# FFN up products by Strassen's algorithm, and the down products after them

## The chip, the core and the metric
One core of a Trainium2 chip runs the kernel. The metric is the device time of one execution in microseconds. Five engines matter: TensorE (PE, with its weight loads PEld), VectorE (DVE), ScalarE (ACT), GpSimd (POOL) and the DMA queue of SyncE (SP). Each works through its own instructions in order and waits for the others by semaphores.

## The reference
One layer over 1024 frames of 1024 channels, in float32; both FFNs have 2816 inner channels:

```
x = x + 0.5 * swiglu(rmsnorm(x, norm_ffn1), wg1, wu1, wd1)
h = rmsnorm(x, norm_mix)
x_m, z_m, x_r, y_r = split(h @ w_in)
mixed = [rmsnorm(mlstm_group(x_m, z_m)), rmsnorm(rglru_group(x_r, y_r))]
x = x + mixed @ w_out
x = x + 0.5 * swiglu(rmsnorm(x, norm_ffn2), wg2, wu2, wd2)
out = rmsnorm(x, norm_final)
swiglu(x, wg, wu, wd) = (silu(x @ wg) * (x @ wu)) @ wd
```

The change is in the two `swiglu` and in how x passes into and out of them.

## The kernel before
Channels lie on the 128 partitions, frames on the free axis: x is eight tiles of 128 x 1024 (`xs`, two tiles of four), each in two halves of 512 frames. A float32 value is split into two parts, hi by a cast on ACT (L105) and lo = value - hi by DVE or POOL (L106); a product is the sum of three passes, hi*hi, hi*lo, lo*hi (`PASSES`), each a matmul of 128 x 128 weights against 128 x 512 values. So a projection of one row of 128 inner channels is 2 halves x 8 tiles x 3 = 48 matmuls (`project`, L285).

An FFN has 22 rows of 128 inner channels. `up_pair` does two of them: gate by L285, times the frames' reciprocal root mean square `rb` on DVE (L330), silu on ACT (L331), times `rb` on POOL (L332), up by L285, the product on DVE (L334) and the split of the result. The norm is late: the products run on x times the gain (`hT`, made by `split_scaled`, L109 on ACT and L110 on DVE), and `rb` is applied to their results. `rb` comes from the squares of x added up in `acc` (L175 on ACT, L177 on POOL or DVE), four small matmuls for each half (L146), a division on DVE (L149, `ms`), a power on POOL (L138), two parts on DVE (L153, L154), two diagonal matrices on DVE (L162), two matmuls that spread the result over the partitions (L165) and a copy on ACT (L166). `defer` and `tick` set where in PE's order these matmuls come: a number of product groups later.

`down` is interleaved with `up_pair`: after every second pair of rows, the rows of the pair before are multiplied with the down weights (L302) and added to x in place (L345); the last call takes four rows. Weights are loaded by SP into `raw` and split into `wu`. In FFN1 the loads of x and the first weights set the pace; in FFN2, `hT` is made while the output projection of the mixer still runs, and L285 matmuls stand between its parts and the statistics.

Of the kernel before, what the change touches and what calls it, by code (L numbers as in the profile page):

```python
# [12 lines left out]
P = 128  # L13
# [20 lines left out]
def hymba_block_kernel(ctx: ExitStack, tc, xT, chv, qkv, kblk, wgate, bgate, up1, dn1, up2, dn2,  # L34
# [13 lines left out]
    r_d = [dram.tile([P, T], F32, name=f"r_d{i}") for i in range(NK)]  # L48
    m_d = dram.tile([H, T], F32, name="m_d")
# [48 lines left out]
    def t2(pool):  # L98
        return pool.tile([P, 512], F32, tag="t2", name="t2", bufs=4)
# [81 lines left out]
    def defer(n, fn):  # L181

        waiting.append([n, fn])
# [16 lines left out]
    class Norm:  # L200
# [3 lines left out]
        def __init__(self, pool, gain, late=False):  # L204
            self.pool, self.gain, self.late, self.acc = pool, gain, late, [[], []]
            self.hT = self.rb = None

# [73 lines left out]

    def project_half(ps, w, hT, half):
# [35 lines left out]
    def ffn(pool, xs, norm, up, dn, after, ahead=(), load_next=lambda: None, last_pieces=halves):  # L318
        hT, rb = norm.hT, norm.rb
        ahead = list(ahead)  # L320

        def up_weights(i):
            return ahead[i] if i < len(ahead) else weights(up[i])

        def up_pair(g):
            res = []
            for f in (2 * g, 2 * g + 1):
                pg = project(up_weights(2 * f), hT)
                s = t4(pool)
# [3 lines left out]
                pu = project(up_weights(2 * f + 1), hT)  # L333
                nc.vector.tensor_tensor(out=s, in0=s, in1=pu, op=ALU.mult)  # L334
                gt = pair(pool, "u8")
                split(gt[:, 0], gt[:, 1], s)
                res.append(gt)
            return res

        def down(fs, acts, last):  # L340
            pieces = last_pieces if last else halves

            def apply(m, h, ps):
                xt = row(xs, m)[:, pieces[h]]
                nc.vector.scalar_tensor_tensor(out=xt, in0=ps, scalar=0.5, in1=xt,  # L345
                                               op0=ALU.mult, op1=ALU.add)
                if last:
                    after(m, h)
            rows = [weights(dn[f]) for f in fs]
            if last:  # L350
                load_next()
            contract(rows, acts, apply, last, pieces)

        last = NF // 2 - 1
        pending = []
        for g in range(last + 1):
            pending += up_pair(g)
            if g == 0:
                open_psum(2, 4)
            if 0 < g < last:  # L360
                down((2 * g - 2, 2 * g - 1), pending[:2], False)
                pending = pending[2:]
        down(range(2 * last - 2, 2 * last + 2), pending, True)


# [6 lines left out]
    open_psum(3, 2)  # L372
    with tc.tile_pool(name="f1", bufs=4, reuse_waits="tile") as pool:
        norm = Norm(nrm, "n1", True)
        ahead = []
        for h in range(2):
            for m in range(NK):
                nc.sync.dma_start(out=row(xs, m)[:, half_of(h)], in_=xT[m, :, half_of(h)])
                norm.scale(xs, m, h)
                if h == 0 and m % 4 == 0:  # L380
                    ahead.append((weights if m else weights_by_half)(up1[m // 4]))
        for h in range(2):
            for m in range(NK):
                norm.square(xs, m, h, 1, (nc.gpsimd, nc.vector)[h])
# [739 lines left out]
```

## Time and profile before

| what | us |
| --- | --- |
| median of 3 runs | 2249.03 |
| lowest and highest | 2248.6, 2249.38 |
| the profiled execution | 2248.25 |
| its span, first to last instruction | 2246.5 |
| PE busy | 2202.3 (98%) |
| DVE busy | 1110.4 (49%) |
| ACT busy | 663.4 (30%) |
| POOL busy | 365.2 (16%) |

The granted clock of TensorE is 0.997 of full speed in the mean. A busy time is the sum over an engine's instructions, also where it works in the shadow of another; what counts is the engine that the end of a stage waits for. FFN1 runs from the start to about 730 us, the mixer to about 1490 us, FFN2 from there to the end.

### The profile page before, as it was taken

Reading aid. Unit: us, or ns where it says so; the run is one execution under the profiler, and the core shown is the slowest. Engines: PE = TensorE matmul, PEld = TensorE weight load, DVE = VectorE, ACT = ScalarE, POOL = GpSimd, SP = SyncE. Lnnn points to the kernel's source line nnn. Section 1 sums busy time; section 2 is a strip of 40 time slices with the busy share of each in tenths; the row PEclk is TensorE's granted clock in tenths of the full one; section 3 lists DMA queues with packets and bytes.
Section 4 is the critical chain, followed back from the end, with each engine's and each line's share of the span. In section 5 each row is a group of like instructions: output and inputs, shape, how many; then the busy total and the mean of one; then the engine's idle time right before and its main releaser. Section 6 shows DMA issues by size and latency. Waiting matters only on the chain.

```text
span 2246.5 us, 24257 instructions
## 1 busy us (share of the span) xinstructions
PE 2202.3 (98%) x10102; PEld 1816.0 (81%) x10102; DVE 1110.4 (49%) x1567; ACT 663.4 (30%) x865; POOL 365.2 (16%) x217
## 2 busy tenths in 40 slices
PE   7999999999999999999999999999999999999998
PEld 5888888888888788878788887777888888888887
DVE  6334344333443645665538999873433334343334
ACT  5111111111112445555546554242111111111114
POOL 3000000000002301232311113431000000000004
PEclk9999999999999999999999999999999999999999
DMA  4111111111112312132246322211111111111102
GB/s 172 55 47 47 48 47 40 54 57 47 47 57 72 116 40 66 64 103 85 85 169 207 104 66 76 71 33 56 47 38 57 47 49 55 47 47 38 57 19 75
DMA packets 62069, 152.12 MB, mean 68 GB/s; under 512 B 5380, under 2 KB 24068, under 8 KB 60936
## 3 DMA queue, kind: packets, MB, share of 16 engines
q1 hardware_dynamic: 61960, 150.58, 20.6%
q8 instruction: 79, 1.29, 0.2%
q14 instruction: 30, 0.25, 0.0%
HBM read 124.85 MB, written 25.71 MB: 67 GB/s over the span
## 4 chain that ended last, share of the span: by engine, by line
PE 86%; DVE 7%; issue 2%; POOL 2%; ACT 1%; DMA 0%; SPq 0%; POOLq 0%; DVEq 0%; ACTq 0%
PE bank_a L285 54%; PE bank_b L302 23%; PE bank_s L302 3%; PE bank_a L531 2%; PE bank_s L808 1%; PE bank_b L837 1%; DVE wu L106 1%; DVE xs L962 1%; DVE hT L110 1%; DVE t L239 1%; DVE w L952 1%; POOL r L138 1%; PE bank_b L634 0%; PE bank_b L619 0%; PE bank_b L616 0%
## 5 line engine op out<-in xcount | busy, mean ns | idle before, releaser
L285 PE MATMUL bank_a<-hT,wu 128*128 128x512 f32 x5712 | 1313.3, 390 | 14.6 <-ACT wu L105 6.2
L285 PEld LDWEIGHTS bank_a<-hT,wu 128*128 128x128 f32 x5712 | 1070.3, 188 | 245.1 <-DVE hT L110 8.1
L302 PE MATMUL bank_b<-u,wu 128*128 128x512 f32 (+1 forms) x2496 | 555.2, 382 | 2.5 <-DVE xs L345 1.3
L302 PEld LDWEIGHTS bank_b<-u,wu 128*128 128x128 f32 x2496 | 456.9, 189 | 95.8 <-DVE xs L962 3.3
L105 ACT CAST wu<-raw 128x1024 fp32r<-128x1024 f32 (+1 forms) x183 | 188.5, 1045 | 1118.5 <-PE bank_a L285 548.1
L345 DVE SCALAR_TENSOR_TENSOR xs<-bank_b,xs 128x512 f32<-128x512 f32 (+1 forms) x328 | 220.1, 677 | 178.7 <-PE bank_b L302 177.1
L332 POOL TENSOR_TENSOR t<-t,rb_late 128x1024 f32<-128x1024 f32 x44 | 105.4, 2396 | 1202.4 <-ACT t L331 1202.4
L106 DVE TENSOR_TENSOR wu<-raw,wu 128x1024 fp32r<-128x1024 f32 (+1 forms) x183 | 226.5, 1247 | 56.8 <-ACT wu L105 56.8
L334 DVE TENSOR_TENSOR t<-t,bank_a 128x1024 f32<-128x1024 f32 x44 | 53.8, 1222 | 366.2 <-PE bank_a L285 362.6
L330 DVE TENSOR_TENSOR t<-rb_late,bank_a 128x1024 f32<-128x1024 f32 x44 | 53.7, 1221 | 311.4 <-PE bank_a L285 309.9
L302 PE MATMUL bank_s<-wu 128*128 128x512 f32 x384 | 97.9, 396 | 3.1 <-ACT wu L105 2.3
L302 PEld LDWEIGHTS bank_s<-wu 128*128 128x128 f32 x384 | 69.5, 188 | 18.6 <-ACT wu L105 3.2
L497 DVE SCALAR_TENSOR_TENSOR t<-bank_a,ch,t 128x1023 f32<-128x1023 f32 (+2 forms) x48 | 61.4, 1278 | 46.0 <-ACT t L494 45.5
L177 POOL TENSOR_TENSOR acc<-acc,t 128x512 f32<-128x512 f32 (+1 forms) x47 | 63.5, 1351 | 109.7 <-ACT t L175 59.3
L105 ACT CAST u<-t 128x1024 fp32r<-128x1024 f32 (+1 forms) x56 | 57.2, 1021 | 26.1 <-DVE t L334 13.5
L808 PE MATMUL bank_s<-q,k 128*128 128x512 f32 (+3 forms) x288 | 61.0, 345 | 0.6 <-DVE q L106 0.6
L837 PE MATMUL bank_b<-v,pc 128*128 128x258 f32 x432 | 61.0, 284 | 0.0
L837 PEld LDWEIGHTS bank_b<-v,pc 128*128 128x128 f32 x432 | 58.0, 190 | 2.7
L106 DVE TENSOR_TENSOR u<-t,u 128x1024 fp32r<-128x1024 f32 x44 | 53.8, 1222 | 1.1 <-ACT u L105 1.1
L808 PEld LDWEIGHTS bank_s<-q,k 128*128 128x128 f32 x288 | 47.7, 189 | 7.8 <-DVE q L106 1.4
L962 DVE TENSOR_TENSOR xs<-xs,bank_b 128x512 f32<-128x512 f32 x64 | 42.7, 681 | 16.5 <-PE bank_b L302 16.3
L331 ACT ACTIVATE t<-t 128x1024 f32<-128x1024 f32 x44 | 46.7, 1062 | 7.6 <-DVE t L330 7.6
(207 smaller groups left out, 1366.3 us busy)
## 6 DMA issues: line engine op xcount, KB each, us to landing
raw<-in_up_dram SPq DMA_DIRECT2D x87, 512.0 KB, 3.6
raw<-in_dn_dram SPq DMA_DIRECT2D x44, 512.0 KB, 3.5
raw<-in_win_dram SPq DMA_DIRECT2D x32, 512.0 KB, 3.6
v_d<-u SPq DMA_DIRECT2D x8, 1024.0 KB, 3.8
v<-v_d SPq DMA_DIRECT2D x16, 512.0 KB, 7.0
raw<-in_wout_dram SPq DMA_DIRECT2D x16, 512.0 KB, 3.6
xs<-in_xT_dram SPq DMA_DIRECT2D x16, 256.0 KB, 5.4
x_d<-xs SPq DMA_DIRECT2D x16, 256.0 KB, 2.0
```

Of the source, the lines that this page charges most:

```text
L105: nc.scalar.copy(hi, src)
L106: (eng or nc.vector).tensor_tensor(out=lo, in0=src, in1=hi.bitcast(F32), op=ALU.subtract)
L177: eng.tensor_tensor(out=box[0], in0=box[0], in1=sq, op=ALU.add)
L285: nc.tensor.matmul(ps, lhsT=w[:, a, k * P:(k + 1) * P], rhs=hT[b][half][:, k], start=(k == 0 and n == 0), stop=(k == NK - 1 and n == 2))
L302: nc.tensor.matmul(ps, lhsT=w[:, a, m * P:(m + 1) * P], rhs=u[:, b, pieces[h]], start=(i == 0 and n == 0), stop=(i == len(lhs) - 1 and n = ...
L332: nc.gpsimd.tensor_tensor(out=s, in0=s, in1=rb, op=ALU.mult)
L334: nc.vector.tensor_tensor(out=s, in0=s, in1=pu, op=ALU.mult)
L345: nc.vector.scalar_tensor_tensor(out=xt, in0=ps, scalar=0.5, in1=xt, op0=ALU.mult, op1=ALU.add)
L497: nc.vector.scalar_tensor_tensor(out=y[:, s:], in0=ps[:, :T - s], scalar=chan(f"{name}c{3 - s}", c), in1=y[:, s:], op0=ALU.mult, op1=ALU.add)
L808: nc.tensor.matmul(s[:, o:], lhsT=hd["k"][:, j, a, J * P:(J + 1) * P], rhs=hd["q"][:, j, b, ih * 512 + o:(ih + 1) * 512], start=(j == 0 an ...
L837: nc.tensor.matmul(st["av"][u][:, 0:258], lhsT=pc[:, a, u * P:(u + 1) * P], rhs=v[:, b, J, 0:258], start=(J == js[0] and n == 0), stop=(J ...
L962: nc.vector.tensor_tensor(out=xt, in0=xt, in1=ps, op=ALU.add)
```

## The change
Of an FFN's 22 rows two (`PLAIN`) are projected as before, with the first half of gate and up interleaved (`project_halves`). Each of the other 20 is taken as a product of 2 x 2 blocks: the gate weights and the up weights are the two block rows, their halves over the input channels the block columns, and the normalised x has 2 x 2 blocks of four tiles by 512 frames. By Strassen's algorithm in Winograd's form that product takes seven block products of 12 matmuls (`block_product`, L394) where the plain way takes eight. `Mixed` makes the seven right-hand operands once for each FFN: x is normalised in place on DVE (L348), differences of its blocks are formed on DVE or POOL (L355), and each is split (`bop`, L106 and L107). For each row, POOL forms four sums of weight halves (L447 to L450), which are split like weights; partial results are kept by three ACT copies out of PSUM (L472) and three DVE adds (L485, L489, L492); the products of silu and up are made by POOL (L497) and DVE (L498) and stored to `u_d` in DRAM.

The down products follow when all rows are done, in groups of 5, 4, 4, 4 and 5 rows; silu(gate)*up comes back from `u_d` and is split then. x, which was overwritten, is loaded again into new tiles (`middle`), in FFN2 from `x_d`, to which the last output products now store it. `t2` has three buffers instead of four. In the up phase PSUM has eight banks of one kind. FFN2's first weights are no longer loaded ahead into a tile of their own.

```diff
-        return pool.tile([P, 512], F32, tag="t2", name="t2", bufs=4)
+        return pool.tile([P, 512], F32, tag="t2", name="t2", bufs=3)
...
+    def project_halves(pss, ws, hT, half):
+
+        for k in range(NK):
+            for ps, w in zip(pss, ws):
+                for n, (a, b) in enumerate(PASSES):
+                    nc.tensor.matmul(ps, lhsT=w[:, a, k * P:(k + 1) * P], rhs=hT[b][half][:, k],
+                                     start=(k == 0 and n == 0), stop=(k == NK - 1 and n == 2))
...
+        def half_ready(self, h):
+            (q11, q12), (q21, q22) = self.q
+            if h == 0:
+                self.steps += [lambda: self.normalize(0, 0),
+                               lambda: self.operand("B11", q11, self.bx),
+                               lambda: self.normalize(1, 0)]
+                return
+            dve, pool = nc.vector, nc.gpsimd
+            self.steps += [lambda: self.normalize(0, 1),
+                           lambda: self.combine(q11, q12, q11, dve),
+                           lambda: self.operand("T1", q11, self.bx),
+                           lambda: self.normalize(1, 1),
+                           lambda: self.combine(q11, q22, q11, dve),
+                           lambda: self.operand("T2", q11, self.bx),
+                           lambda: self.combine(q12, q22, q12, pool),
+                           lambda: self.operand("B21", q21, bigp, pool),
+                           lambda: self.operand("T3", q12, bigp),
+                           lambda: self.combine(q21, q21, q11, pool),
+                           lambda: self.operand("B22", q22, bigp, pool),
+                           lambda: self.operand("T4", q21, bigp)]
...
+    def block_product(ps, w, u, first):
...
+        for k in range(4):
+            for n, (a, b) in enumerate(PASSES):
+                nc.tensor.matmul(ps, lhsT=w[:, a, k * P:(k + 1) * P], rhs=u[:, b, k],
+                                 start=(first and k == 0 and n == 0),
+                                 stop=(k == 3 and n == 2), skip_group_check=not first)
+        tick()
+
+    PLAIN = 2
+    GROUPS = (5, 4, 4, 4, 5)
...
+            def sums(self):
+                self.s, self.z = raw_tile(), raw_tile()
+                lo, hi = half_of(0), half_of(1)
+                add = nc.gpsimd.tensor_tensor
+                add(out=self.s[:, lo], in0=self.u[:, lo], in1=self.u[:, hi], op=ALU.add)
+                add(out=self.s[:, hi], in0=self.s[:, lo], in1=self.g[:, lo], op=ALU.subtract)
+                add(out=self.z[:, lo], in0=self.g[:, lo], in1=self.u[:, lo], op=ALU.subtract)
+                add(out=self.z[:, hi], in0=self.g[:, hi], in1=self.s[:, hi], op=ALU.subtract)
...
+            block_product(X, p.wg[:, :, lo], B["B11"], True)
+            g1 = kept(X)
+            after(0)
+            block_product(Y, p.ws[:, :, lo], B["T1"], True)
+            u2 = kept(Y)
+            after(1)
+            block_product(X, p.ws[:, :, hi], B["T2"], False)
+            g2 = kept(X)
+            after(2)
+            Z = bank_b()
+            block_product(Z, p.wg[:, :, hi], B["B21"], True)
+            nc.vector.tensor_tensor(out=g1, in0=g1, in1=Z, op=ALU.add)
+            nc.scalar.activation(g1, g1, AF.Silu)
+            after(3)
+            block_product(X, p.wz[:, :, lo], B["T3"], False)
+            nc.vector.tensor_tensor(out=u2, in0=u2, in1=X, op=ALU.add)
+            after(4)
+            block_product(Y, p.wz[:, :, hi], B["B22"], False)
+            nc.vector.tensor_tensor(out=g2, in0=g2, in1=Y, op=ALU.add)
+            nc.scalar.activation(g2, g2, AF.Silu)
+            after(5)
+            block_product(X, p.wu, B["T4"], False)
+            o1, o2 = t2(norm.pool), t2(norm.pool)
+            nc.gpsimd.tensor_tensor(out=o2, in0=g2, in1=u2, op=ALU.mult)
+            nc.vector.tensor_tensor(out=o1, in0=g1, in1=X, op=ALU.mult)
+            store(p.f, 0, o1)
+            store(p.f, 1, o2)
+            after(6)
...
+                for f in products([rows[f] for f in fs], [acts[f] for f in fs], apply, last, pieces):
+                    f()
+                    if ahead:
+                        ahead.pop(0)()
...
+    for h in range(2):
+        for m in range(NK):
+            norm.square(xs, m, h, 1, (nc.gpsimd, nc.vector)[h], (1, 4)[h])
```

The order of PE around the statistics of FFN1's first half, before. A row is a line, an operation, the tile written and read, the shape and the count.

```order
L285 MATMUL bank_a<-hT,wu 128x512 [waits DVE_49]
L146 MATMUL bank_b<-ones_r,acc 128x2 [waits Pool_49]
L146 MATMUL bank_b<-ones_r,acc 128x2 x3
L285 MATMUL bank_a<-hT,wu 128x512 x28
L146 MATMUL bank_b<-ones_r,acc 128x2 [waits DVE_49]
L146 MATMUL bank_b<-ones_r,acc 128x2 x3
L165 MATMUL bank_b<-t_324,ones_r 128x512 [waits PE_49]
L165 MATMUL bank_b<-t_327,ones_r 128x512
```

And in the changed kernel, at the same place:

```order
L292 MATMUL bank_b<-hT,wu 128x512 x4
L147 MATMUL bank_b<-ones_r,acc 128x2 [waits Pool_49]
L147 MATMUL bank_b<-ones_r,acc 128x2 x3
L166 MATMUL bank_b<-t_345,ones_r 128x512 [waits DVE_49]
L300 MATMUL bank_b<-hT,wu 128x512
L166 MATMUL bank_b<-t_348,ones_r 128x512 [waits DVE_49]
L300 MATMUL bank_b<-hT,wu 128x512 x23
```

The 28 projection matmuls between the statistics and their spreading are gone, and the second half's statistics come later.

The order of ACT where the changed kernel goes from the plain rows to the block products in FFN1; `bop` are the operands, the last two of them T4's, and `ct` the copies out of PSUM:

```order
L106 CAST bop<-xs 128x1024 [waits DVE_49]
L106 CAST bop<-xs 128x1024 [waits PE_49,Pool_49]
L106 CAST bop<-xs 128x1024 [waits Pool_49]
L472 COPY ct<-bank_b 128x512 [waits DMAHW1_49,PE_49]
L472 COPY ct<-bank_b 128x512 [waits DMAHW2_49,PE_49]
L106 CAST wu<-raw 128x1024 [waits DMAHW0_49]
L472 COPY ct<-bank_b 128x512 [waits DMAHW4_49,PE_49]
```

The copies that free X and Y stand behind the casts of the last operand, which wait for POOL. POOL's own order there, from the first difference on:

```order
L355 TENSOR_TENSOR xs<-xs 128x2x512 [waits DVE_49] x2
L429 TENSOR_TENSOR ct<-ct,rb_late 128x512 [waits Activation_49]
L447 TENSOR_TENSOR raw<-raw 128x512 [waits DMAHW3_49,DVE_49,Pool_49]
L448 TENSOR_TENSOR raw<-raw 128x512 [waits DMAHW0_49,Pool_49]
L449 TENSOR_TENSOR raw<-raw 128x512 [waits DVE_49]
L450 TENSOR_TENSOR raw<-raw 128x512 [waits Pool_49]
L355 TENSOR_TENSOR xs<-xs 128x2x512 [waits DVE_49]
L107 TENSOR_TENSOR bop<-xs,bop 128x1024 [waits Activation_49]
L355 TENSOR_TENSOR xs<-xs 128x2x512 [waits DVE_49]
```

The weight sums of the second Strassen row stand between the differences; none of these instructions is in the kernel before.

The order of DVE in the changed kernel ahead of the second half's statistics of FFN2:

```order
L178 TENSOR_TENSOR acc<-acc,t_10928 128x512 [waits Activation_49,Pool_49]
L107 TENSOR_TENSOR wu<-raw,wu 128x1024 [waits DMAHW0_49,Activation_49]
L348 SCALAR_TENSOR_TENSOR xs<-xs,ch,rb_late 128x512 [waits DMAHW5_49]
L348 SCALAR_TENSOR_TENSOR xs<-xs,ch,rb_late 128x512 [waits DMAHW6_49]
L107 TENSOR_TENSOR bop<-xs,bop 128x1024 [waits Activation_49]
L348 SCALAR_TENSOR_TENSOR xs<-xs,ch,rb_late 128x512 [waits DMAHW7_49]
L107 TENSOR_TENSOR bop<-xs,bop 128x1024 [waits Activation_49]
L348 SCALAR_TENSOR_TENSOR xs<-xs,ch,rb_late 128x512 [waits DMAHW0_49]
L348 SCALAR_TENSOR_TENSOR xs<-xs,ch,rb_late 128x512 [waits DMAHW1_49]
L348 SCALAR_TENSOR_TENSOR xs<-xs,ch,rb_late 128x512 [waits DMAHW2_49]
L427 TENSOR_TENSOR ct<-rb_late,bank_b 128x512 [waits PE_49]
L150 TENSOR_SCALAR ms<-bank_b 128x4 [waits PE_49]
```

Before, `ms` (L149) followed the last accumulator add (L177) with one weight split between them; now the normalising of the first half and two operand splits stand there as well.

## Rows read from the trace of the kernel before

**Rows 1.** The page's first part: engine, busy us, share, instructions.
```profile
PE 2202.3 (98%) x10102; PEld 1816.0 (81%) x10102; DVE 1110.4 (49%) x1567; ACT 663.4 (30%) x865; POOL 365.2 (16%) x217
```
**Rows 2.** The chain that ended last: its share of the span by engine.
```profile
PE 86%; DVE 7%; issue 2%; POOL 2%; ACT 1%; DMA 0%; SPq 0%; POOLq 0%; DVEq 0%; ACTq 0%
```
**Rows 3.** Windows: stretch, length, busy us of PE, PEld, DVE, ACT, POOL, clock, DMA.
```profile
300.00:400.00 100.00, 100.00 (x443) 82.77 (x442) 41.38 (x49) 14.57 (x14) 4.79 (x2) 1.00 0.14 48
1560.00:2200.00 640.00, 640.00 (x2824) 529.65 (x2823) 238.09 (x266) 107.88 (x106) 51.34 (x23) 1.00 0.15 45
```
**Rows 4.** Timeline of PE near the end: start, length, work, count.
```profile
2219.58 7.11 PE L302 MATMUL bank_b<-u,wu 128*128 128x256 f32 x58
```
**Rows 5.** Groups by shape: line, engine, work, count | busy us, mean ns | idle before.
```profile
L332 POOL TENSOR_TENSOR t<-t,rb_late 128x1024 f32<-128x1024 f32 x44 | 105.4, 2396 | 1202.4 <-ACT t L331 1202.4
L177 POOL TENSOR_TENSOR acc<-acc,t 128x512 f32<-128x512 f32 x37 | 55.6, 1502 | 101.1 <-ACT t L175 50.8 <-issue 49.3
L110 DVE SCALAR_TENSOR_TENSOR hT<-xs,ch,hT 128x512 fp32r<-128x512 f32 x32 | 34.8, 1119 | 4.9 <-ACT hT L109 4.9
L138 POOL TENSOR_TENSOR r<-ms,mhalf 128x4 f32<-128x4 f32 x11 | 14.5, 1314 | 70.9 <-DVE ms L149 70.9
L106 DVE TENSOR_TENSOR yp<-t,yp 128x1024 fp32r<-128x1024 f32 x8 | 12.3, 1542 | 17.8 <-ACT yp L105 17.8
L166 ACT COPY rb_late<-bank_b 128x512 f32<-128x512 f32 x4 | 2.4, 588 | 12.6 <-PE bank_b L165 12.6
```
**Rows 6.** The page's costliest groups, the same columns.
```profile
L285 PEld LDWEIGHTS bank_a<-hT,wu 128*128 128x128 f32 x5712 | 1070.3, 188 | 245.1 <-DVE hT L110 8.1
...
L105 ACT CAST wu<-raw 128x1024 fp32r<-128x1024 f32 (+1 forms) x183 | 188.5, 1045 | 1118.5 <-PE bank_a L285 548.1
L345 DVE SCALAR_TENSOR_TENSOR xs<-bank_b,xs 128x512 f32<-128x512 f32 (+1 forms) x328 | 220.1, 677 | 178.7 <-PE bank_b L302 177.1
...
L106 DVE TENSOR_TENSOR wu<-raw,wu 128x1024 fp32r<-128x1024 f32 (+1 forms) x183 | 226.5, 1247 | 56.8 <-ACT wu L105 56.8
```
**Rows 7.** The page's DMA issues: work, count, KB, us to landing.
```profile
raw<-in_up_dram SPq DMA_DIRECT2D x87, 512.0 KB, 3.6
...
x_d<-xs SPq DMA_DIRECT2D x16, 256.0 KB, 2.0
```
**Rows 8.** Timeline of PE in FFN1's start, with the idle time before in brackets.
```profile
27.35 0.95 PE L146 MATMUL bank_b<-ones_r,acc 128*128 128x2 f32 x8
...
35.63 1.05 PE L146 MATMUL bank_b<-ones_r,acc 128*128 128x2 f32 x8 [0.88 <-DVE acc L177]
```
**Rows 9.** Windows of L285 alone: PE busy (count), PEld, clock, DMA.
```profile
0.00:36.50 36.50, 23.62 (x83) 15.40 (x83) 1.00 0.56 204
1489.00:1534.30 45.30, 23.87 (x100) 18.90 (x101) 0.92 0.07 24
```
**Rows 10.** Timeline of DVE in FFN1's start.
```profile
21.23 5.10 DVE L110 SCALAR_TENSOR_TENSOR hT<-xs,ch,hT 128x512 fp32r<-128x512 f32 x6
...
33.09 0.69 DVE L162 TENSOR_TENSOR t<-ident,parts 128x512 fp32r<-128x512 f32 x1
```
**Rows 11.** Timeline of PE at the start of FFN2.
```profile
1489.69 3.19 PE L285 MATMUL bank_a<-hT,wu 128*128 128x512 f32 x13
1495.29 1.87 PE L146 MATMUL bank_b<-ones_r,acc 128*128 128x2 f32 x8 [2.41 <-DVE acc L177]
1497.02 5.17 PE L302 MATMUL bank_b<-u,wu 128*128 128x512 f32 x12
...
1519.09 1.05 PE L146 MATMUL bank_b<-ones_r,acc 128*128 128x2 f32 x8 [1.80 <-DVE acc L177]
...
1523.43 16.75 PE L285 MATMUL bank_a<-hT,wu 128*128 128x512 f32 x73
```
**Rows 12.** Windows of all engines, columns as in rows 3.
```profile
2.00:6.00 4.00, 0.00 (x0) 0.00 (x0) 0.75 (x1) 1.86 (x5) 0.00 (x0) 1.00 0.87 272
...
1494.00:1502.00 8.00, 6.71 (x20) 5.69 (x21) 3.08 (x7) 2.07 (x4) 1.09 (x2) 0.57 0.00 0
```

More of the change, by code (lines that the diff above doesn't have):

```diff
@@ L48, in hymba_block_kernel @@
     r_d = [dram.tile([P, T], F32, name=f"r_d{i}") for i in range(NK)]
+    u_d = [dram.tile([P, T], F32, name=f"u_d{i}") for i in range(NF)]
     m_d = dram.tile([H, T], F32, name="m_d")
@@ L354, in ffn, with __init__, load, split_g @@
[L354 to L363, printed above, removed]
+                store(f, h, s)
+        class Pair:
+            def __init__(self, f):
+                self.f = f
+            def load(self):
+                self.g, self.u = load(up[2 * self.f]), load(up[2 * self.f + 1])
+            def sums(self):
[6 more added lines that the diff above has]
+                add(out=self.z[:, hi], in0=self.g[:, hi], in1=self.s[:, hi], op=ALU.subtract)
+            def split_g(self):
+                self.wg = weights(None, loaded=self.g)
+            def split_s(self):
+                self.ws = weights(None, loaded=self.s)
+            def split_z(self):
+                self.wz = weights(None, loaded=self.z)
+            def split_u(self):
+                self.wu = pool.tile([P, 2, 512], R32, tag="wd", name="wd", bufs=1)
+                split(self.wu[:, 0], self.wu[:, 1], self.u[:, half_of(1)])
@@ new lines, in run, with kept @@
+        def run(p, after):
+            B = mixed.ops
+            X, Y = bank_b(), bank_b()
+            lo, hi = half_of(0), half_of(1)
+            def kept(ps):
+                t = ct()
+                nc.scalar.copy(t, ps)
+                return t
+            block_product(X, p.wg[:, :, lo], B["B11"], True)
[26 more added lines that the diff above has]
+            after(6)
@@ new lines, in up_phase, with after @@
+        pairs = [Pair(f) for f in range(PLAIN, NF)]
+        first = pairs[0]
+        first.load()
+        first.sums()
+        first.split_g()
+        first.split_s()
+        first.split_z()
+        first.split_u()
+        mixed.step(99)
+        for n, p in enumerate(pairs):
+            nxt = pairs[n + 1] if n + 1 < len(pairs) else None
+            def after(i):
+                if nxt is None:
+                    return last_pair(i)
+                if i == 0:
+                    nxt.load()
+                elif i == 1:
+                    nxt.sums()
+                elif i == 2:
+                    nxt.split_g()
+                elif i == 4:
+                    nxt.split_s()
+                elif i == 5:
+                    nxt.split_z()
+                elif i == 6:
+                    nxt.split_u()
+            run(p, after)
+            if n == len(pairs) - 5:
+                middle()
```

196 lines of the change are left out of this document (141 added, 55 removed).

## The prediction
> **What bounds the kernel now.** I read the page's first part first: PE is busy 2202.3 us of a span of 2246.5 [rows 1]. The chain of work that ended last agrees: 86% of it is PE [rows 2]. Then the windows, to see how dense the FFN stages are: 443 matmuls in 100 us, 2824 in 640 us, PE busy for the whole of either, granted clock 1.00 [rows 3]. So a 512-column matmul costs 100/443 = 0.2257 us there and nothing waits. Every matmul that goes is worth 0.2257 us, unless the new order makes PE wait. DVE is 41% busy in such a window, ACT 15%, POOL 5%: there is room, but what is asked of it comes in chains.
>
> PE idles 2246.5 - 2202.3 = 44 us in all, mostly at the few places where a norm's statistics go through PE. Those are the places where the change moves instructions, so they are read one by one below.
>
> **What goes.** Twenty of the 22 pairs of each FFN take seven block products of 12 matmuls where there were eight: 40 x 12 = 480 matmuls fewer, 480 x 0.2257 = 108.3 us. With the last down group five rows long instead of four, 24 matmuls of 512 columns become 48 of 256; 58 of those took 7.11 us [rows 4], 0.123 each, so 48 x 0.123 - 24 x 0.2257 = +0.5. The gain is **107.8 us** if PE waits no more than now.
>
> **The steady pair loop.** A pair is 84 matmuls, 18.96 us of PE. Beside it POOL does four weight sums and one product of 512 columns, 5 x 1.50 = 7.5 us by the accumulator adds [rows 5]; ACT does three casts of 1.05, a smaller one, three copies of 0.59 and two silus no dearer than the casts, under 8 us [rows 5, 6]; DVE three splits of 1.25, one of about 0.7 and four PSUM operations of 0.68, 7.2 us [rows 6]. All lie under 18.96. In latency the tightest link that I find is the add that reads X between the fifth and the seventh product (L489): the sixth product gives it 12 x 0.2257 = 2.71 us, it takes 0.68, which leaves about 2 us. The copies of X and Y have one product as well, and weights are loaded (3.6 us to landing [rows 7]), summed and split most of a pair ahead. I take the loop's loss as 0; up to 0.5 us a pair (20 us) goes into the range, since no row shows such a run of small hand-overs.
>
> **Start of FFN1.** Before, the statistics of the first half go through PE at 27.35, those of the second at 35.63 [rows 8], and PE has done 83 L285 matmuls by 36.5 [rows 9]. The new order has only 48 matmuls (gate and up of the first half) ahead of the first half's L147, and directly behind it the L166 that spreads the result. That L166 waits for a diagonal (L163) on DVE, which stands there behind the second half's hT, six accumulator adds and a split. Before, hT ended at 21.23 + 5.10 = 26.3 and the first diagonal began at 33.09, with four of those adds ahead of it [rows 10]. The new queue holds about the same, so I put the diagonal's end at 33.8, the second one's at 35, PE's restart at 35.5. By 36.86 it will have done some 54 matmuls instead of 83: 29 x 0.2257 = 6.5 us lost. PE has by then stood for some 10 us.
>
> What such a wait does to the clock has a row: after 2.41 us of idle before the statistics at 1495.29 the granted clock was 0.57 over 8 us [rows 11, 12], so mostly at the lower level of 1.2 GHz, and 12 L302 matmuls took 5.17 us where 12 x 0.2257 = 2.7 [rows 11]: 2.5 us lost. I charge 2.5 us for each new wait of several us. The Trainium skill ("TensorE: Matmul & The Clock Gate", Part 1) says that the default state is throttled and that activity releases it; the fall at 1495 agrees, while the window from 2 to 6 us has clock 1.00 without one matmul [rows 12], which does not. By that rule the restart would cost what 1495 cost; if the chip's behaviour at the kernel's start held here too, the sum would be 2.5 lower. With my charge, the start of FFN1 costs **9 us** (4 to 13).
>
> **From plain to Strassen in FFN1.** After the second half is spread (t1), 72 plain matmuls are left, 16.3 us. In that time DVE and POOL must normalise the second half (eight L348, 1.12 each beside a busy POOL, as L110 [rows 5]), form the differences and split the operands. Two splits and three of the differences are POOL's, in pieces of 1024 columns at 2.40 (as L332 [rows 5]). POOL gets its first difference's input at about t1 + 13: eight L348 are 9.0, and two differences and a PSUM operation lie between them on DVE. Its queue then runs: two pieces 4.8, a product 1.5, four weight sums 6.0, then three pieces 7.2, to t1 + 32. The last of these gates the second T4 cast, and in ACT's queue both T4 casts stand ahead of the first copy of X (L472). The third product accumulates into X, so it waits for that copy: t1 + 32 + 1.05 + 0.59, near t1 + 34. Until then PE has the 16.3 us, two products (5.4) and what does not need X of the fourth, up to t1 + 22 or 23. The loss is about 10.5 us (5 to 15 by how the POOL pieces overlap), plus 2.5 of clock: **13 us** (3, if POOL's pieces are all done early, to 18).
>
> **Start of FFN2.** Before, 100 L285 matmuls are done between 1489 and 1534.3 [rows 9], laid in part between the statistics, 73 in one run from 1523.43 [rows 11]. In the new order 48 gate and up matmuls stand together behind the output projection, then the second half's L147, and directly its L166. On DVE the `ms` for it stands behind a weight split, six L348, two operand splits and an L427: from 1521 on (before, these statistics came at 1519.09 [rows 11]; two L348 now stand ahead) 1.25 + 6 x 1.0 (L110's 1.12 at times when POOL is busy) + 2.5 + 0.7 = 10.5, so 1531.5; then POOL's power (1.31 [rows 5]) and the first diagonal, so PE restarts near 1534 with 48 done instead of some 98: 50 x 0.2257 = 11 us lost, plus 2.5 of clock: **13 us** (6 to 17). The switch to Strassen there has up to 144 plain matmuls (32.5 us) ahead of it, enough for the T4 work: 0 (to 2).
>
> **The rest.** Entering the down groups, the reloads of x and of silu(gate)*up (stores land in 2.0 us, loads in 3.6 [rows 7]), three `t2` buffers instead of four at the norms, the last statistics: no row shows what they will cost; four places, 0 to 3 us each, **4 us** taken. A gain there I exclude, since each adds a wait and takes none away. The middle (projections, mLSTM, RG-LRU) keeps its PE order: 0.
>
> **Sum.** The profiled execution took 2248.25: 2248.25 - 107.8 + 9 + 13 + 13 + 4 = 2179.5. The median of the three runs stands 0.8 above it, so **2180 us**.
>
> **Rivals.**
> (a) *The covers hold.* POOL and DVE get through their queues as fast as PE needs: 4 + 3 + 6 at the three places and 3 for the rest, 2249.0 - 107.8 + 16 = 2157. For it: every engine but PE is under half busy. Against: at these places the order decides, not the load, and the queues above are first in, first out. Chance 0.14.
> (b) *The pair loop binds a little.* One link in the loop is 0.5 to 1.2 us late, 40 pairs give +20 to +48: 2200 to 2228. For it: beside a busy POOL DVE has slow rows, L106 `yp` at 1.54 against 1.25 elsewhere [rows 5, 6]. Against: the 2 us of slack, and PE without idle before, with POOL and DVE at work beside each other. Chance 0.18.
> (c) *The pair loop binds so hard that the kernel is slower.* The place: POOL's sums and DVE's splits, on the way to a product's weights. From (2249 - 2180)/40 = 1.7 us a pair on, the gain is gone. If DVE's splits (3 x 1.25 + 0.7 = 4.4 us a pair) held up POOL's operations for their whole length, and the 2 us of slack were all there is, 2.4 us a pair would be missing: 2180 + 96 = 2276. The rows at 1.54 show the two hindering each other by 0.3 us an operation, not by a full block. Chance 0.05, of which 0.01 ends within 0.2% of before. The Trainium skill ("SBUF — State Buffer", SBUF: two separate sides) has a rule that would give such a time: a DVE operation with two SBUF inputs and a GpSimd operation that reads SBUF exclude each other for a whole instruction.
> (d) *The gain is not what it says.* Fewer matmuls but each dearer, for instance by weight loads. Against: these take 188 ns, under 226 [rows 6], and the shapes are the same. Chance 0.01, near 2240.
> (e) *The forecast*: 0.62.
>
> **How the numbers follow.** The stage costs at their low ends together (13) and at their high ends (13 + 18 + 17 + 12 + 2 = 62) would give 2154 and 2203; all at one end is unlikely, and the loop adds to the upper side alone. Range 2157 to 2210: it leaves out the lower part of (a), the upper half of (b), and (c) and (d). A measurement of this kernel can tell about 0.2% from no change. Faster: (a), (b), (d) and (e), 0.95. Within 0.2%: 0.01. Slower: 0.04.
>
> **What would show it.** PE's busy time near 2095 plus what the half clock adds. Windows inside the two up phases: 443 matmuls in 100 us again and no idle; if (b) or (c), idle ahead of L394 that POOL or ACT ends. Two waits of PE at L166, from about 24 to 35 us and about as long in the first 50 us of FFN2, both ended by the diagonal on DVE. One wait of about 10 us at an L394 near 60 us, ended by ACT's copy `ct`, itself behind the `bop` casts that wait for POOL. After each of the three, some us of half clock. The forecast is wrong if those waits are absent or twice as long, or if the loop has regular gaps.

## The result and the profile after

The changed kernel takes 2195.62 us (median of 4 runs, 2193.34 to 2196.43) where the kernel before took 2248.82 (4 runs): a ratio of 0.9763, 95% interval 0.9746 to 0.978. The forecast was 2180 with a range from 2157 to 2210. The profiled execution took 2196.43 us, 51.8 less than the one of before; the forecast for it was 68.8 less. So the saving came, the range held, and the new waits cost 56 us instead of the 39 of the sum.

The page of the changed kernel, first part (busy us of each engine) and the chain that ended last, which answer to [rows 1, 2]:

```profile
PE 2104.9 (96%) x9646; PEld 1735.8 (79%) x9646; DVE 1199.3 (55%) x1635; ACT 824.5 (38%) x1137; POOL 610.0 (28%) x397
...
PE 80%; DVE 10%; ACT 3%; issue 3%; POOL 3%; DMA 2%; SPq 0%; POOLq 0%; DVEq 0%; ACTq 0%
```

PE's busy time fell by 97.4 us, less than 107.8: behind its waits PE runs for some microseconds at half clock, where a matmul is longer. DVE, ACT and POOL now hold a larger part of the chain. What PE waited for, longest first (what waited, for whom: us, times, longest):

```profile
PE bank_b L166 <- DVE t L163: 29.2, 5, 13.8
PE bank_b L394 <- ACT ct L472: 18.6, 2, 17.9
PE bank_b L147 <- DVE acc L178: 6.9, 2, 5.4
```

The two waits at L166 (13.8 and 9.7) and the one at L394 (17.9) are the three that the prediction named, ended by the engines that it named. The one at L394 was forecast at about 10 us near 60 us; it lasts from 85 to 103 us. Windows of the changed kernel, columns as in [rows 3]; the first lies in the Strassen phase of FFN1, the others hold the start, the switch from plain rows to block products, the first matmuls behind the wait in it, and the entry into the down groups:

```profile
200.00:300.00 100.00, 100.00 (x443) 82.82 (x442) 36.02 (x41) 34.21 (x48) 34.73 (x25) 1.00 0.24 83
...
0.00:62.18 62.18, 38.59 (x140) 28.45 (x141) 48.10 (x56) 31.76 (x48) 28.84 (x23) 0.86 0.38 137
62.18:103.33 41.15, 23.17 (x101) 18.50 (x99) 39.19 (x27) 14.47 (x17) 29.68 (x12) 0.83 0.09 28
103.33:118.00 14.67, 14.67 (x58) 12.00 (x59) 9.90 (x8) 6.26 (x9) 5.01 (x4) 0.89 0.76 256
480.00:492.00 12.00, 9.71 (x35) 7.35 (x34) 9.17 (x9) 5.96 (x7) 1.34 (x1) 0.86 0.81 257
```

In the pair loop PE is busy for the whole window (300 to 400 us reads the same), at the 443 matmuls in 100 us of [rows 3]: the loop costs nothing. Up to the end of the wait in the switch, DVE is busy for 39.19 of 41.15 us and POOL for 29.68, while PE does 100 matmuls, worth 22.6 us. PE's timeline there:

```profile
24.23 0.95 PE L147 MATMUL bank_b<-ones_r,acc 128*128 128x2 f32 x8
38.93 0.80 PE L166 MATMUL bank_b<-t,ones_r 128*128 128x512 f32 x1 [13.75 <-DVE t L163]
...
40.72 12.97 PE L300 MATMUL bank_b<-hT,wu 128*128 128x512 f32 x47
...
61.33 1.01 PE L166 MATMUL bank_b<-t,ones_r 128*128 128x512 f32 x2 [1.30 <-DVE t L163]
62.18 16.52 PE L300 MATMUL bank_b<-hT,wu 128*128 128x512 f32 x72
78.54 6.87 PE L394 MATMUL bank_b<-bop,wu 128*128 128x512 f32 x28
103.33 11.84 PE L394 MATMUL bank_b<-bop,wu 128*128 128x512 f32 x44 [17.92 <-ACT ct L472]
```

The 47 matmuls from 40.72 took 12.97 us for 10.6 at full clock, the 44 from 103.33 took 11.84 for 9.9: 2.4 and 1.9 us lost. The granted clock was 0.50 from 30 to 45 us and again from 103.3 to 106 us, that is 1.2 GHz, the lower of its two levels, during and behind the two long waits. What POOL, DVE and ACT did in the switch, some of their rows (start, length, work, count):

```profile
89.64 2.24 POOL L450 TENSOR_TENSOR raw<-raw 128x512 f32<-128x512 f32 x1
91.84 3.32 POOL L355 TENSOR_TENSOR xs<-xs 128x1024 f32<-128x1024 f32 x1
...
98.40 3.31 POOL L355 TENSOR_TENSOR xs<-xs 128x1024 f32<-128x1024 f32 x1
...
101.75 1.04 ACT L106 CAST bop<-xs 128x1024 fp32r<-128x1024 f32 x1 [5.51 <-POOL xs L355]
102.70 1.07 ACT L472 COPY ct<-bank_b 128x512 f32<-128x512 f32 x2
...
88.48 17.63 DVE L107 TENSOR_TENSOR bop<-xs,bop 128x1024 fp32r<-128x1024 f32 x6
```

The chain is the one of the prediction's sum, from POOL's weight sums over T4's cast to the copy of X and the third product. Its pieces are longer: a POOL sum 2.24 us where I took 1.50 [rows 5], a POOL piece of 1024 columns 3.3 where I took 2.40, a DVE split 17.63/6 = 2.94 where the rows have 1.25 [rows 6].

### The profile page after: what moved, and what is told of

It reads as the page before. It is cut to its first block, busy times and chain, and to the rows that moved or that the text cites. A ratio compares the mean times of both kernels' runs of the same rounds, so it can differ in the third digit from the quotient of the medians.

```text
span 2194.7 us, 24662 instructions
## 1 busy us (share of the span) xinstructions
PE 2104.9 (96%) x9646; PEld 1735.8 (79%) x9646; DVE 1199.3 (55%) x1635; ACT 824.5 (38%) x1137; POOL 610.0 (28%) x397
## 4 chain that ended last, share of the span: by engine, by line
PE 80%; DVE 10%; ACT 3%; issue 3%; POOL 3%; DMA 2%; SPq 0%; POOLq 0%; DVEq 0%; ACTq 0%
PE bank_b L394 32%; PE bank_b L317 24%; PE bank_a L300 13%; PE bank_s L317 3%; PE bank_a L780 2%; DVE wu L107 1%; PE bank_s L1057 1%; PE bank_b L300 1%; PE bank_b L1086 1%; DMA raw<-u_d 1%; DVE bop L107 1%; DVE xs L1211 1%; DVE w L1201 1%; DVE hT L111 1%; DVE t L244 1%
## 5 line engine op out<-in xcount | busy, mean ns | idle before, releaser
L394 PE MATMUL bank_b<-bop,wu 128*128 128x512 f32 x2880 | 663.7, 390 | 21.7 <-ACT ct L472 18.6
L394 PEld LDWEIGHTS bank_b<-bop,wu 128*128 128x128 f32 x2880 | 542.4, 189 | 136.5 <-ACT ct L472 19.5
L107 DVE TENSOR_TENSOR wu<-raw,wu 128x1024 fp32r<-128x1024 f32 (+1 forms) x203 | 266.5, 1314 | 391.8 <-ACT wu L106 391.8
L317 PE MATMUL bank_b<-u,wu 128*128 128x512 f32 (+1 forms) x1536 | 347.1, 380 | 3.8 <-DVE wu L107 3.0
L300 PE MATMUL bank_a<-hT,wu 128*128 128x512 f32 x1488 | 345.8, 391 | 3.0 <-ACT t L808 1.4
L106 ACT CAST wu<-raw 128x1024 fp32r<-128x1024 f32 (+1 forms) x203 | 211.2, 1045 | 362.3 <-PE bank_b L394 182.3
L300 PEld LDWEIGHTS bank_a<-hT,wu 128*128 128x128 f32 x1488 | 277.9, 188 | 64.1 <-POOL hT L107 1.9
L317 PEld LDWEIGHTS bank_b<-u,wu 128*128 128x128 f32 x1536 | 279.3, 190 | 60.1 <-DVE wu L107 3.9
L317 PE MATMUL bank_b<-u 128*128 128x512 f32 (+1 forms) x1080 | 253.5, 385 | 1.6 <-POOL u L107 0.9
L598 DVE SCALAR_TENSOR_TENSOR xs<-bank_b,xs 128x512 f32<-128x512 f32 (+1 forms) x168 | 110.9, 664 | 231.4 <-PE bank_b L317 231.3
L317 PEld LDWEIGHTS bank_b<-u 128*128 128x128 f32 x1080 | 200.3, 188 | 42.9 <-POOL u L107 1.7
L472 ACT COPY ct<-bank_b 128x512 f32<-128x512 f32 x120 | 70.2, 587 | 240.5 <-PE bank_b L394 240.5
L447 POOL TENSOR_TENSOR raw<-raw 128x512 f32<-128x512 f32 x40 | 54.2, 1355 | 380.6 <-DMA raw<-in_up_dram 380.6
L394 PE MATMUL bank_b<-bop,wd 128*128 128x512 f32 x480 | 115.6, 390 | 0.5 <-DVE ct L489 0.5
L106 ACT CAST u<-raw 128x1024 fp32r<-128x1024 f32 x66 | 68.4, 1051 | 120.0 <-PE bank_b L317 64.1
L394 PEld LDWEIGHTS bank_b<-bop,wd 128*128 128x128 f32 x480 | 90.0, 188 | 19.9 <-DVE ct L489 1.3
L107 DVE TENSOR_TENSOR u<-raw,u 128x1024 fp32r<-128x1024 f32 x66 | 80.4, 1229 | 36.6 <-ACT u L106 36.2
L497 POOL TENSOR_TENSOR t<-ct 128x512 f32<-128x512 f32 x40 | 74.7, 1866 | 86.9 <-ACT ct L493 86.9
```

What stands on the lines that cost most here:

```text
L106: nc.scalar.copy(hi, src)
L107: (eng or nc.vector).tensor_tensor(out=lo, in0=src, in1=hi.bitcast(F32), op=ALU.subtract)
L300: nc.tensor.matmul(ps, lhsT=w[:, a, k * P:(k + 1) * P], rhs=hT[b][half][:, k], start=(k == 0 and n == 0), stop=(k == NK - 1 and n == 2))
L317: nc.tensor.matmul(ps, lhsT=w[:, a, m * P:(m + 1) * P], rhs=u[:, b, pieces[h]], start=(i == 0 and n == 0), stop=(i == len(lhs) - 1 and n = ...
L394: nc.tensor.matmul(ps, lhsT=w[:, a, k * P:(k + 1) * P], rhs=u[:, b, k], start=(first and k == 0 and n == 0), stop=(k == 3 and n == 2), ski ...
L447: add(out=self.s[:, lo], in0=self.u[:, lo], in1=self.u[:, hi], op=ALU.add)
```

## The experiments

Each run is one or a few edits to the changed kernel; times are medians of 4 runs. "The spread" is L166, which lays the norm of a half over the partitions; "cover" is the plain matmuls that PE can do while the operands are made.

**Is it ACT's queue? (e1)** The last three operand steps are issued behind the third copy of the first pair:

```diff
-        mixed.step(99)
+        mixed.step(len(mixed.steps) - 3)
...
                 elif i == 2:
+                    mixed.step(99)
                     nxt.split_g()
```

> One edit to the changed kernel: the last three operand steps (the difference for T4, B22, T4) are issued inside the first Strassen pair, after its third copy, instead of ahead of it. On ACT the first copy of X then stands ahead of both T4 casts, the other two copies still behind them. Theory Q (the wait of 17.9 us at the third product of FFN1 is ACT's queue: the copy stands behind casts that wait for POOL): the third and fourth product run at once and the wait moves to the fifth; the POOL chain ends as late as now, so the gain is two products, 2 x 2.7 = 5.4 us, 2190 us. Theory R (the third product really waits for POOL or DVE work of its own operands, T2): no change, 2195.6. FFN2 unchanged in both.

2190.03 us, 5.6 less, as theory Q said. PE's timeline:

```profile
78.43 5.93 PE L394 MATMUL bank_b<-bop,wu 128*128 128x512 f32 x24
90.03 3.58 PE L394 MATMUL bank_b<-bop,wu 128*128 128x512 f32 x7 [5.66 <-ACT ct L472]
96.17 5.76 PE L394 MATMUL bank_b<-bop,wu 128*128 128x512 f32 x17 [2.57 <-DVE bop L107]
104.72 7.09 PE L394 MATMUL bank_b<-bop,wu 128*128 128x512 f32 x24 [2.79 <-ACT ct L472]
```

The third product still waits for its copy, 5.7 us instead of 17.9, and no longer for the end of POOL's chain; the fifth does that (24 + 7 + 17 = 48 matmuls ahead of it), at 104.7 where the third stood at 103.3. Two products were gained: the queue is a cause, and behind it the length of the operand work is the bound.

**Is it POOL and DVE holding each other up? (e2)** The operands' differences and splits go to DVE alone:

```diff
-                           lambda: self.combine(q12, q22, q12, pool),
-                           lambda: self.operand("B21", q21, bigp, pool),
+                           lambda: self.combine(q12, q22, q12, dve),
+                           lambda: self.operand("B21", q21, bigp),
...
-                           lambda: self.combine(q21, q21, q11, pool),
-                           lambda: self.operand("B22", q22, bigp, pool),
+                           lambda: self.combine(q21, q21, q11, dve),
+                           lambda: self.operand("B22", q22, bigp),
```

> One edit to the changed kernel: the differences and splits of the operands that POOL made (four pieces of differences, four of splits in each FFN) are made by DVE; POOL keeps weight sums and products. Theory L (POOL and DVE hold each other up piece by piece while both run, so POOL's share brings nothing): the DVE pieces fall from about 2.9 to 1.25 us, all operands are done by about 100 us as now or earlier, the copies are not blocked, FFN1 gains 10 to 13 us and FFN2 2 to 4: 2179 to 2184. Theory P (POOL works in parallel and only the queues are badly ordered): DVE has 8 more pieces, 10 us, behind the same start, T4 comes some 10 us later, and the time is 2195 to 2206.

2175.23 us (2171.82 to 2179.44), 20.4 less; theory P is out, and the median is even 4 us below theory L's range. With 8 more pieces in each FFN DVE is done sooner. Groups by shape (count | busy us, mean ns | idle before), from 60 to 120 us of the changed kernel:

```profile
L107 DVE TENSOR_TENSOR bop<-xs,bop 128x1024 fp32r<-128x1024 f32 x8 | 20.0, 2544 | 0.7 <-ACT bop L106 0.7
...
L355 DVE TENSOR_TENSOR xs<-xs 128x1024 f32<-128x1024 f32 x4 | 6.4, 1610 | 0.0
```

and of this run:

```profile
L107 DVE TENSOR_TENSOR bop<-xs,bop 128x1024 fp32r<-128x1024 f32 x10 | 14.0, 1428 | 0.0
L355 DVE TENSOR_TENSOR xs<-xs 128x1024 f32<-128x1024 f32 x8 | 11.2, 1411 | 0.0
```

PE's timeline of this run:

```profile
76.70 5.60 PE L394 MATMUL bank_b<-bop,wu 128*128 128x512 f32 x24
83.57 0.49 PE L394 MATMUL bank_b<-bop,wu 128*128 128x512 f32 x1 [1.27 <-ACT ct L472]
84.23 1.65 PE L394 MATMUL bank_b<-bop,wu 128*128 128x512 f32 x6 [0.16 <-DVE bop L107]
88.67 13.68 PE L394 MATMUL bank_b<-bop,wu 128*128 128x512 f32 x52 [2.79 <-DVE bop L107]
```

12 pieces took 26.4 us, 18 take 25.2. Within this run, too, three of DVE's pieces of 1024 columns take 2.29 to 2.31 us while POOL's weight sums run (79.6 to 87.5 us), and the six behind them 1.21 each. The wait of 17.9 us is down to 4.2. That the engines hold each other up is shown; how much of the 20.4 us it is worth is not. The copies stand in another place of ACT's queue here (e1 gives 5.6 us for a part of that queue), and POOL's weight sums no longer stand ahead of any difference, which no run tried alone.

**Is it the cover? (e3)** A third row is projected plainly, right ahead of the first pair:

```diff
+        rows = [weights(up[2 * PLAIN]), weights(up[2 * PLAIN + 1])]
+        for h in range(2):
+            pg, pu = bank_b(), bank_b()
+            for ps, w in ((pg, rows[0]), (pu, rows[1])):
+                project_half(ps, w, norm.hT, h)
...
-        pairs = [Pair(f) for f in range(PLAIN, NF)]
+        pairs = [Pair(f) for f in range(PLAIN + 1, NF)]
```

> One edit to the changed kernel: a third row of each FFN is projected plainly, both halves, right ahead of the first Strassen pair: 96 matmuls (21.7 us) more between the second spreading of the norm and the block products, and 2 x 12 = 24 matmuls more in all. Theory C (the switch is a fixed 41 to 44 us of DVE and POOL work that PE has to cover; it had 22 us of cover in FFN1 and 38 in FFN2): the waits of 17.9 us in FFN1 and 4.3 us in FFN2 go, with about 2 us of half clock, and 5.4 us of matmuls come: 2195.6 - 24 + 5.4 = 2177. If the wait does not hang on the cover, the time rises by the 5.4 us to 2201.

2177.65 us, the expected time, but not by the expected way. PE's timeline in FFN1:

```profile
34.00 0.79 PE L166 MATMUL bank_b<-t,ones_r 128*128 128x512 f32 x1 [9.48 <-DVE t L163]
...
93.65 5.60 PE L394 MATMUL bank_b<-bop,wu 128*128 128x512 f32 x24
109.93 2.50 PE L394 MATMUL bank_b<-bop,wu 128*128 128x512 f32 x5 [10.68 <-ACT ct L485]
```

The wait at the third product is still 10.7 us, 54 us behind the spread: theory C's fixed length falls. ACT's queue holds the copies back here too: the cast of an operand waits 10.25 us for POOL's difference, up to 103.10, and the copies come at 109.31, behind it and five more casts. The operands' tiles come from the pool that holds hT, which the third row reads to its end; whether this is what makes POOL and ACT late was not tried apart. And a part of the gain is at the start, where L166 waits 9.5 us instead of 13.8: the order of POOL's work changed, and the first pair's weight sums no longer lie there.

**The same sums alone (e8).** They are held back until the first half is spread:

```diff
-            def sums(self):
+            def sums(self, behind=None):
...
+                if behind is not None:
+                    nc.gpsimd.tensor_copy(self.s[:, 0:1], behind)
+                    nc.gpsimd.tensor_copy(self.z[:, 0:1], behind)
...
-        first.sums()
+        first.sums(norm.rb[:, 0:1])
```

> One edit to the changed kernel: POOL's four weight sums of the first Strassen pair are held back until the first half of the norm has been spread, by a copy of one column of the spread result ahead of them into the tiles that they write (overwritten by the sums); in FFN1 they now run from about 29.6 to 36.3 us beside DVE's accumulator adds. Theory L (while POOL runs such a sum, DVE's instructions are held up, also the small ones: casts of 4 columns took 1.24 us there): DVE reaches the diagonal at about 33.3 instead of 38.2, PE's wait at L166 shrinks from 13.8 to 9 us, and 3 to 5 us of it last to the end: 2191 to 2193. Theory N (DVE's delay there has another cause, such as the split of wd or ACT's squares): no change in the wait, 2195.6.

2197.38 us, no gain, although the wait shrank as theory L says. DVE in the changed kernel, and POOL beside it:

```profile
29.93 1.24 DVE L154 CAST parts<-r 128x4 fp32r<-128x4 f32 x1
...
29.61 1.53 POOL L447 TENSOR_TENSOR raw<-raw 128x512 f32<-128x512 f32 x1
31.11 1.79 POOL L449 TENSOR_TENSOR raw<-raw 128x512 f32<-128x512 f32 x1
```

in this run DVE, then PE:

```profile
30.15 0.16 DVE L154 CAST parts<-r 128x4 fp32r<-128x4 f32 x1
...
35.28 0.80 PE L166 MATMUL bank_b<-t,ones_r 128*128 128x512 f32 x1 [9.88 <-DVE t L163]
...
60.98 1.30 PE L166 MATMUL bank_b<-t,ones_r 128*128 128x512 f32 x2 [4.99 <-DVE t L163]
```

and DVE behind the first spread, in this run and in e3, where no weight sum runs beside it:

```profile
37.94 4.82 DVE L348 SCALAR_TENSOR_TENSOR xs<-xs,ch,rb_late 128x512 f32<-128x512 f32 x4 [1.50 <-ACT rb_late L167]
...
43.27 3.94 DVE L107 TENSOR_TENSOR bop<-xs,bop 128x1024 fp32r<-128x1024 f32 x2
```

```profile
36.65 2.74 DVE L348 SCALAR_TENSOR_TENSOR xs<-xs,ch,rb_late 128x512 f32<-128x512 f32 x4 [0.90 <-ACT rb_late L167]
...
39.91 2.35 DVE L107 TENSOR_TENSOR bop<-xs,bop 128x1024 fp32r<-128x1024 f32 x2
```

With the sums away the instruction of 4 columns takes 0.16 us instead of 1.24; beside the sum it had ended at 31.17, with the sum itself (31.14). PE restarts 3.7 us earlier, and waits 3.7 us longer at the second half's L166, which comes at 61 us in both kernels. The sums are not gone, though: they now run from 38.7 to 46.1 us, and DVE's six pieces beside them take 3.7 us longer than in e3. In e3, whose POOL does neither these sums nor operand splits ahead of the second spread, that spread comes at 55.0 us. So e8 shows that the sums hold DVE up at either place; it does not show what the start would cost without them.

**Filler at the start of FFN1 (e4).** L166 of the first half comes 48 matmuls later, behind the second row's gate and up, and the first row's silu and products follow then:

```diff
+                if h == 0 and f < wait_rows:
+                    continue
...
-            norm.square(xs, m, h, 1, (nc.gpsimd, nc.vector)[h], (1, 4)[h])
+            norm.square(xs, m, h, (3, 1)[h], (nc.gpsimd, nc.vector)[h], (1, 4)[h])
```

> One edit to the changed kernel: in FFN1 the first half's statistics are spread (L166) 48 plain matmuls later, behind gate and up of the second row, and the first row's silu and products follow then. Theory F (the 13.8 us of PE's wait at L166 near 25 us is the missing filler): 10.8 us of matmuls move into the wait, about 2 us of half clock go, and the switch to Strassen starts some 10 us earlier, since its DVE work can: 2183 to 2186. Theory G (DVE is the bound from 25 us to the end of the switch, so the gain is given back at the third product): the wait there grows from 17.9 to 25 us and more, and the time stays at 2193 to 2196.

2187.74 us, 7.9 less, between theory F's range and theory G's. The second spread comes at 48.5 instead of 61.3, 12.8 earlier; some 5 us are given back in the switch:

```profile
86.02 1.65 PE L394 MATMUL bank_b<-bop,wu 128*128 128x512 f32 x3 [7.72 <-ACT bop L106]
94.00 2.93 PE L394 MATMUL bank_b<-bop,wu 128*128 128x512 f32 x6 [6.33 <-DVE bop L107]
```

**The same filler at the start of FFN2 (e5).** The second half's spread comes 48 matmuls later (`wait1 = 3`):

```diff
-            self.square(xs, m, h, 2 if h == 0 else 1)
+            self.square(xs, m, h, 2 if h == 0 else self.wait1)
...
+        norm.wait1 = 3
```

> One edit to the changed kernel: in FFN2 the second half's statistics are spread 48 plain matmuls later (behind the second row's gate and up instead of directly behind the sums). Theory F (the 9.7 us that PE waits at L166 there are missing filler): the wait goes, with some 2 us of half clock, and the time falls to 2184. Theory G (the spread hangs on DVE and not on PE, and what DVE and POOL then need until the block products can run, about 44 us from the spread, stays): 10.8 us of cover move ahead of the spread and are missing behind it, so the waits at L394 in FFN2 grow from 4.3 us by 7 to 10, and the time is 2192 to 2197.

2194.6 us, theory G. First the changed kernel, then this run:

```profile
1478.32 4.83 PE L317 MATMUL bank_b<-u,wu 128*128 128x512 f32 x12
...
1516.48 0.79 PE L166 MATMUL bank_b<-t,ones_r 128*128 128x512 f32 x1 [9.71 <-DVE t L163]
...
1518.36 33.05 PE L300 MATMUL bank_b<-hT,wu 128*128 128x512 f32 x142
...
1557.93 3.87 PE L394 MATMUL bank_b<-bop,wu 128*128 128x512 f32 x10 [1.85 <-DVE wu L107]
```

```profile
1517.10 0.62 PE L166 MATMUL bank_b<-t,ones_r 128*128 128x512 f32 x2
1517.55 21.94 PE L301 MATMUL bank_b<-hT,wu 128*128 128x512 f32 x96
...
1553.89 12.35 PE L395 MATMUL bank_b<-bop,wu 128*128 128x512 f32 x43 [7.43 <-ACT ct L473]
```

The wait of 9.7 us at L166 is gone and comes back as 7.4 at L395 with smaller ones around it: what DVE and POOL still have to do behind the spread is the same, with 48 matmuls less to cover it.

**What is a matmul worth? (e7)** An eighth block product is added to each pair, its result read by nobody:

```diff
+            block_product(bank_b(), p.wu, B["T4"], True)
             block_product(X, p.wu, B["T4"], False)
```

> One addition to the changed kernel: an eighth block product (12 matmuls on T4 into a spare bank whose result nobody reads) in each of the 40 Strassen pairs, so 480 matmuls more, as many as the algorithm saves; the rest stays. Theory PE (in the pair loop PE alone sets the pace, each matmul is worth 0.2257 us): 2195.6 + 108.3 = 2304. Rival (some of the loop's time is another engine's and hides added matmuls, so the saving was never worth its full price): clearly less, under 2290.

2301.23 us, 105.6 more for 480 matmuls, 0.220 each, 98% of the price. With them PE is again busy for the whole of 200 to 400 us, at 443 matmuls in 100 us. PE alone sets the pace of the loop; the saving of the change is worth what was put into the sum, to 3 us.

**Together (e6, e9, e10).** DVE alone with both fills, then with the third row, and the third row with DVE alone but no fill:

> Three edits together: operands on DVE alone (as e2_dve_only, 2175.2), the fill in FFN1 (as e4_fill_ffn1, 8 us gained) and the fill in FFN2 (as e5_fill_ffn2). If the gains add because DVE, freed of POOL's blocking, has its operands done well before PE needs them: 2175 - 8 - 9 = 2158. If DVE becomes the bound at the switch and gives the fills back: 2167 to 2175.

> e6_dve_and_fill (2165.6) with the third plain row of e3_third_plain. The row's 24 matmuls more cost 5.4 us in the two FFNs. In e6 PE still waits 11 us in FFN1 and 7 us in FFN2 between the spread and the end of the first Strassen pair. If the 96 matmuls of cover hide these: 2165.6 + 5.4 - 16 = 2155 to 2158. If the third row holds the hT buffers, whose place B22 and T4 take, to its end, so that their casts, splits and the copies of X and Y queued behind them move along with it: little gain, 2163 to 2168.

> e2_dve_only (2175.2) with the third plain row of e3_third_plain, without the fills. e2 gained 20.4 us and e3 18.0 us over the changed kernel. If both took away the same waits, the sum of both is no better than e2 alone with 5.4 us of matmuls added and its last 4 to 6 us of waits gone: 2173 to 2177. If they took away different ones: 2195.6 - 20.4 - 18.0 = 2157.

2165.62, 2160.19 and 2170.02 us. In the first, some of the fill is given back at the switch, where PE waits 6.8 us for an operand's cast in FFN1 and 7.0 for a copy in FFN2 (the branch of the smaller gain, a little better than it said). The third row takes another 5.4 us from it, between the two branches. In the last, e2 and e3 have mostly the same waits to take: 2170.02 is nearer to the first branch (2173 to 2177) than to 2157. What is left in the second of the three, FFN1:

```profile
42.95 38.43 PE L301 MATMUL bank_b<-hT,wu 128*128 128x512 f32 x168
...
99.40 12.79 PE L395 MATMUL bank_b<-bop,wu 128*128 128x512 f32 x48 [12.58 <-ACT ct L493]
```

Even with 168 plain matmuls behind the spread the third product waits 12.6 us for the copy of X. This version is the fastest tried, 0.9612 of the kernel before (0.9596 to 0.9628).

## Why the prediction was right in its mechanism and short in its sizes

| term of the sum | forecast us (range) | measured us | from |
| --- | --- | --- | --- |
| 480 matmuls | 108.3 | 105.6 for 480 added | e7 |
| pair loop | 0 (to 20) | 0 | windows of the changed kernel |
| start of FFN1 | 9 (4 to 13) | 15.8 | 190 plain matmuls by 62.18 before, 120 now: 70 x 0.2257 |
| switch in FFN1 | 13 (3 to 18) | 20.2 | 41.15 + 14.67 us for 158 matmuls (35.7) |
| start of FFN2 | 13 (6 to 17) | 14.0 | 50 plain matmuls by 1518.36 now; before, 112 by 1537.07, which is 18.7 us later, as the first statistics are: 62 x 0.2257 |
| switch in FFN2 | 0 (to 2) | 7.7 | 58.7 us (1518.36 to 1577.07) for 226 matmuls (51.0) |
| the rest | 4 (0 to 12) | about 1 | some 4 at the first down group, some 3 gained in the middle |

The measured costs add up to 59 us; the difference of the two profiled executions leaves 107.8 - 51.8 = 56, and the 3 us between the two are not placed. Three terms lie above their own ranges. That the total stays within 2157 to 2210 is in part luck: the range left room on its upper side for a pair loop that then cost nothing, and FFN2's start and the rest stayed inside their ranges.

**The saving and the loop** came as forecast. Rival (b) and rival (c), with a loop that binds, are refuted by the windows of the Strassen phase, and rival (d) by e7. Rival (a), with covers that hold, is refuted by the three waits.

**Start of FFN1.** The order was read rightly, PE restarted at 38.9 instead of 35.5. The step that failed is "the new queue holds about the same": it left out that POOL's weight sums for the first Strassen pair run at that time and hold up DVE (e8: 38.9 back to 35.3). It also read four adds ahead of the first diagonal where the trace of before has five. The other part of the 6.8 us missing is that the count stopped at 36.86, ahead of the second half's statistics and their wait of 1.3 us, which the kernel before had behind it by 42 us. That second spread the sum did not price: POOL's two operand splits stand around its power there, and DVE's 4-column cast beside the second of them takes 2.35 us (e3: 0.17).

**Switch in FFN1.** The queue that I followed through POOL and ACT is the one in the trace, and its t1 + 34 came as 103.33 - 62.18 = 41 us. The term that was mis-sized is the price of a POOL piece beside a busy DVE: 2.24 and 3.3 us instead of 1.50 and 2.40. The prediction took both prices as means over the kernel before, in which DVE is busy for half of the span [rows 1], and it used the 0.3 us an operation of rival (c) as the measure of the hindrance. Where both engines work without a pause, DVE's split is at 2.94 for 1.25. The rule of the Trainium skill ("SBUF — State Buffer", SBUF: two separate sides), that a DVE operation with two SBUF inputs and a GpSimd operation that reads SBUF exclude each other for a whole instruction, was weighed against the pair loop, where there was time for it; it belonged here. The runs agree with it for the splits (e2: 2.29 us beside POOL's sums, 1.21 behind them). The 4-column cast of e8 has one input; the same passage also names DVE operations in a 2-port mode, and whether this cast runs in one, no run here shows.

**Start of FFN2** was sized rightly, 14 for 13. **The switch in FFN2** was taken as covered by 144 matmuls; it took some 44 us and 7.7 were lost. The same mis-sized price has a part in it: with POOL's pieces on DVE (e2) the same 226 matmuls take 55.2 us instead of 58.7. What the rest is stays open. e5 shows that this cover had nothing to spare.

**The half clock** was charged with 2.5 us for each of the three new waits. It cost 2.4 and 1.9 in FFN1, but behind the third wait, at 1518.36, the 142 matmuls took 33.05 us for 32.05, so 1.0. The close 2.4 is in part luck: behind the first wait the same 47 matmuls took 11.74 us in e1 and 13.02 in e3, a loss of 1.1 to 2.4. The fall behind FFN2's first statistics is no new cost: 12 matmuls took 4.83 us there as they had taken 5.17 before [rows 11].

What the prediction read as a disagreement, a clock of 1.00 from 2 to 6 us without one matmul [rows 12], is none. The first clock that the trace of before holds is for 10.07 us, and the profile prints 1.00 where it holds none. The matmuls tell the level. In the changed kernel, whose first clock is for 14.53 us, those from 12.1 to 14.3 us began 0.43 us apart, as behind the 7.7 us wait of e4 at a granted clock of 0.50, and those from 14.6 us on 0.23 us apart. In the kernel before, the closest ahead of 10.07 us are 0.43 us apart as well. So both kernels started at the lower level, and there was nothing at the start by which the sum could have been 2.5 lower.

## What to carry to other kernels

A saving of matmuls in a loop that PE fills is worth its count times its price; what decides the rest is the few microseconds in which the loop is entered, and these are read from the order of each engine's queue, not from its load, at the prices that hold beside busy neighbours. A piece given to POOL to relieve DVE can cost both: price such pieces from a stretch where both engines work without a pause. Work that is moved out of a wait can hold up its neighbours again where it lands (e8). A wait that is filled may come back at the next place that the same engine bounds, so before filling one, find what ends last behind it.

## What was not expected of the hardware

POOL beside a busy DVE took 2.24 us for 512 columns and 3.3 for 1024, where the rows of before have 1.50 and 2.40; DVE's two-input split of 1024 columns took 2.94 instead of 1.25, and its 4-column cast 1.24 instead of 0.16. Twelve DVE pieces with POOL's help lasted longer (26.4 us) than eighteen without (25.2). Both kernels began at the lower clock level, though the profile prints 1.00 there.
